# Final norm with sixteen buffers and its loads first; layer 1 projection with an early second load and squares and high parts on two engines

## The chip, the cores and the metric

The kernel runs on one core of one Trainium2 chip. The metric is device time in microseconds (us) of one execution. Before the change it is 3293.6 us, the median of three runs (3292.09 to 3293.63).

## What is computed

A trunk of two layers over 2048 tokens of width 1024 in float32. Layer 0 mixes tokens with causal pooling and a convolution, layer 1 with a chunked gated delta rule over 8 heads; each is followed by a mixture of 32 experts (2 per token). Every sub-layer starts with a normalization whose gain and shift come from a conditioning vector, and the output is normalized once more:

```python
def rmsnorm(x, gain):
    xf = x.astype(jnp.float32)
    y = xf * lax.rsqrt(jnp.mean(xf * xf, axis=-1, keepdims=True) + EPS)
    return (y * gain.astype(jnp.float32)).astype(x.dtype)
...
        mod = (c_act @ mod_w[l] + mod_b[l])[:, None, :]
        sh_m, sc_m, g_m, sh_f, sc_f, g_f = jnp.split(mod, 6, axis=-1)
        hn = rmsnorm(x, norm_mix[l]) * (1.0 + sc_m) + sh_m
...
    return rmsnorm(x, final_norm)
```

In layer 1 the normalized tokens are multiplied with a weight of 1024 x 4112: 4096 columns for queries, keys, values and a gate of 8 heads, and 16 columns for two numbers per head and token.

## The kernel before

The program runs in stages: layer 0's mixer, its experts, layer 1's mixer, its experts, and `final`. Tokens are cut into 16 tiles of 128; four tiles make a chunk of 512, two chunks a half. Float32 products are made from a high part (float32r) and a low part: `split` writes the high part of a tile with a copy on ScalarE (or on VectorE, if told so) and the low part with a subtraction on VectorE, and `proj` multiplies high by high, high by low and low by high.

**Final norm** (`final`, L1038). For each of 16 tiles: load from `acc` (L1045, `xin`, six buffers), square and sum on ScalarE (L1048), mean on VectorE and power on POOL (`rstd`, L187 and L189), scaling by the row's factor and by the gain row `fr` on VectorE (L1050), store (L1051). Loads and stores are issued by SP, which works through its queue in order.

**Layer 1's projection** (`dn_project`, L1130). It has two halves. In each, for both chunks: `norm_x` (L202) loads four tiles of x (L1157, `xin`, four buffers), squares and sums each on ScalarE (L210), takes the power (L189), and scales the tiles on VectorE (L217). `norm_T` (L220) then makes, for each of 8 slices of 128 features, four transposes on TensorE (L229), the scaled and shifted tile `nf` on ScalarE (L231, two buffers), its high part `hh` on ScalarE (L232), its low part `hl` on VectorE (L233). The 16 columns are multiplied at once (L1174), `gates` makes the heads' factors from them, and then come 8 heads (`dn_head`). A head loads four strips of weights (`load_strip`, L244), splits each and multiplies it with both chunks; between the strips `pump` (L1190) advances other work: a triangular inverse, and one block of the modulation (`mod_rest`, L160), which loads 128 rows of its weight (`modw`, L167), multiplies and sums them with the condition on VectorE (L168) and adds a bias (L169). The first call also loads the condition and applies Silu to it. There are 32 such blocks and four calls per head.

The order of instructions on an engine is made by a scheduler of the Tile library from the order of the program and the dependencies, with times of its own. `tc.issue_after(ins)` adds to it: instructions traced in its block are queued behind `ins` if they run on the engine of `ins`. The buffers of the heads' results `na` and `kg` (L1291, L1303) are 8 KB per partition each, in the pool `last`. `first` (L1162) holds the tiles of the third chunk, which `norm_x` prepares ahead of head 7 (L1184).

Of the kernel before, what the change touches and what calls it, by code (L numbers as in the profile page):

```python
# [6 lines left out]
F32 = mybir.dt.float32  # L7
# [63 lines left out]
class Trunk:  # L71
# [127 lines left out]
                nc.tensor.transpose(p[:, j * P:(j + 1) * P], src[:, k:k + 1].to_broadcast([P, P]), self.ident)  # L199
            nc.scalar.activation(out[:, h * 512:(h + 1) * 512], p, AF.Copy)  # L200

    def norm_x(self, l, xload, wk):  # L202

        nc = self.nc
        ss = self.small.tile([P, 4], F32, name="ss")
        xs = []
        for i in range(4):
            x = xload(i)
            sq = wk.tile([P, D], BF16, name="sq", tag="nf", bufs=2)
            nc.scalar.activation(sq, x, AF.Square, accum_out=ss[:, i:i + 1])  # L210
            xs.append(x)
        r = self.rstd(ss, 1.0 / D, 4, "rs")
        for i in range(4):
            if l == 0:
                nc.scalar.activation(xs[i], xs[i], AF.Copy, scale=r[:, i:i + 1])
            else:
                nc.vector.tensor_scalar(xs[i], xs[i], r[:, i:i + 1], None, op0=ALU.mult)  # L217
        return xs

    def norm_T(self, l, which, xs, psum, wk, outs):  # L220

        nc = self.nc
        hh, hl = outs
        g = self.gain[l, which]
        so = l * 48 + (0 if which == 0 else 3) * 8
        for k in range(KD):
            p = psum.tile([P, 512], F32, name="tp")
            for i in range(4):
                nc.tensor.transpose(p[:, i * P:(i + 1) * P], xs[i][:, k * P:(k + 1) * P], self.ident)  # L229
            f = wk.tile([P, 512], F32, name="nf", bufs=2)  # L230
            nc.scalar.activation(f, p, AF.Identity, scale=g[:, k:k + 1], bias=self.mod[:, so + k:so + k + 1])  # L231
            nc.scalar.activation(hh[:, k], f, AF.Copy)  # L232
            nc.vector.tensor_sub(hl[:, k], f, hh[:, k].bitcast(F32))  # L233

    def split(self, h, l, x, eng="act"):
        nc = self.nc
# [801 lines left out]
    def final(self, out, l=1):  # L1038
        tc, nc = self.tc, self.nc
        with tc.tile_pool(name="fin", bufs=3, reuse_waits="tile") as pool:  # L1040
            fr = pool.tile([P, D], F32, name="fr", bufs=1)
            nc.sync.dma_start(fr, self.ins["final"].to_broadcast([P, D]))  # L1042
            for t in range(NT):
                x = pool.tile([P, D], F32, name="xin", bufs=6)
                nc.sync.dma_start(x, self.acc[t * P:(t + 1) * P])  # L1045
                ss = self.small.tile([P, 1], F32, name="ss1")
                sq = pool.tile([P, D], BF16, name="sqo", bufs=1)
                nc.scalar.activation(sq, x, AF.Square, accum_out=ss)  # L1048
                r = self.rstd(ss, 1.0 / D, 1, "rs1")
                nc.vector.scalar_tensor_tensor(x, x, r, fr, op0=ALU.mult, op1=ALU.mult)  # L1050
                nc.sync.dma_start(out[t * P:(t + 1) * P], x)  # L1051
# [78 lines left out]
    def dn_project(self):  # L1130
# [3 lines left out]
        with ExitStack() as ctx:  # L1134
# [24 lines left out]
                return f  # L1159

            self.rest = self.mod_rest(cv, [(1, i) for i in range(16, 48)], tag="modw", bufs=3)
            first = None  # L1162
            for half in range(2):
                hT = []
                ba = cv.tile([P, 8, 16], F32, name="ba", bufs=2)
                for c2 in range(2):
                    hh = hp.tile([P, KD, 512], F32R, name="hh")
                    hl = hp.tile([P, KD, 512], F32R, name="hl")
                    xs = first or self.norm_x(1, xload(half * 2 + c2), wk)
                    first = None  # L1170
                    self.norm_T(1, 0, xs, pst, wk, (hh, hl))
                    hT.append((hh, hl))
                    p = psm.tile([P, 512], F32, name="pm")
                    self.proj(p[:16], (wbh, wbl), (hh, hl))  # L1174
                    bs = wk.tile([16, 512], F32, name="bs", bufs=1)
                    nc.scalar.activation(bs, p[:16], AF.Copy)
                    p = pst.tile([P, 512], F32, name="tp")
                    for i in range(4):
                        nc.tensor.transpose(p[:, i * 16:(i + 1) * 16], bs[:, i * P:(i + 1) * P], self.ident[:16, :16])
                    nc.vector.tensor_copy(ba[:, c2 * 4:c2 * 4 + 4], p[:, :64].rearrange("p (b c) -> p b c", b=4))  # L1180
                beta, g, ex = self.gates(half, ba, cv, pst)
                for hd in range(8):
                    if (half, hd) == (0, 7):
                        first = self.norm_x(1, xload(2), wk)  # L1184
                    self.dn_head(half, hd, hT, beta, g, ex, halo, wp, wk, psm, pst, psk)
                    if hd % 4 == 3:
                        assert next(self.inv, None) is None
                        self.inv = self.dn_invert(half, hd // 4, wk) if (half, hd) != (1, 7) else iter(())

    def pump(self, n):  # L1190

        for _ in range(n):
            next(self.inv, None)
        with self.tc.issue_after(self.loaded.ins):
            next(self.rest, None)

    def dn_head(self, half, hd, hT, beta, g, ex, halo, wp, wk, psm, pst, psk):
        nc, ins = self.nc, self.ins
# [536 lines left out]
```

## Time and profile before

| | |
|---|---|
| Median of three runs | 3293.6 us |
| Profiled execution, its own time | 3291.32 us |
| Its span | 3289.6 us |
| Mean granted TensorE clock | 0.948 |

The profile is of one execution. Times in it count from the start of the span. PE is TensorE (PEld its weight loads), DVE VectorE, ACT ScalarE, POOL GpSimd, SP the engine that issues most DMAs; a q behind a name is the engine's queue. In a timeline a row has start, duration, engine, line, operation, output<-input, shape and count, and in brackets the idle time before it with what ended it.

### The profile page before, as it was taken

The numbers are of one execution on the slowest core, as the hardware profiler recorded it, in microseconds if no ns is written. First come the engines' busy times: TensorE is split into PE (matmuls) and PEld (weight loads), VectorE is DVE, ScalarE is ACT, GpSimd is POOL, SyncE is SP. The second block draws the span as 40 slices with busy tenths as digits, with TensorE's granted clock in tenths as the row PEclk, the third lists the DMA queues.
The fourth block names the chain that finished last, engine by engine and source line by source line (L and its number), as shares of the span: only waits on it lengthen the run. The fifth ranks groups of instructions, "written<-read, shape, count | busy, mean of one in ns | idle before, by whom it ended". The sixth has DMA issues, their size and how long they took to land. (4 is left out here: it accounts for less than half of the span.)

```text
span 3289.6 us, 41913 instructions
## 1 busy us (share of the span) xinstructions
PE 2900.5 (88%) x14192; PEld 2309.4 (70%) x14192; DVE 2435.8 (74%) x3797; ACT 1493.0 (45%) x2559; POOL 1019.7 (31%) x877
## 2 busy tenths in 40 slices
PE   4979888787999996999988999987999996999991
PEld 3756666565777774888876777867897775777770
DVE  4998999767878875768786786877664547888783
ACT  6135233315656655434345343434673224666552
POOL 0142323333444331323222222235540213444441
PEclk9989999888999997999999999988999997999995
DMA  6225243638999864455442434347877537989876
GB/s 223 85 74 208 77 143 115 218 134 276 314 285 304 257 201 151 150 176 179 144 144 93 133 117 141 112 149 215 257 246 225 171 128 253 319 274 299 263 231 219
DMA packets 384985, 633.38 MB, mean 193 GB/s; under 512 B 111232, under 2 KB 245504, under 8 KB 384768
## 3 DMA queue, kind: packets, MB, share of 16 engines
q1 hardware_dynamic: 355904, 563.38, 50.2%
q0 software_dynamic: 28864, 67.30, 8.8%
q8 instruction: 113, 1.85, 0.2%
q14 instruction: 104, 0.85, 0.1%
HBM read 484.46 MB, written 175.44 MB: 201 GB/s over the span
## 5 line engine op out<-in xcount | busy, mean ns | idle before, releaser
L260 PE MATMUL pm<-hh,wh 128*128 128x512 f32 x1408 | 565.9, 402 | 0.8 <-ACT wh L237 0.7
L262 PE MATMUL pm<-hh,wl 128*128 128x512 f32 x1408 | 556.7, 396 | 3.7 <-DVE wl L238 3.7
L261 PE MATMUL pm<-hl,wh 128*128 128x512 f32 x1408 | 555.6, 395 | 4.1 <-DVE hl L233 4.1
L238 DVE TENSOR_TENSOR wl<-wr,wh 128x1024 fp32r<-128x1024 f32 x384 | 452.3, 1219 | 40.7 <-ACT wh L237 37.2
L237 ACT ACTIVATE wh<-wr 128x1024 fp32r<-128x1024 f32 x384 | 399.3, 1057 | 139.8 <-PE pu L828 57.3
L847 POOL DMA_INDIRECT acc<-ys,ixs x102 | 262.2, 2570 | 436.9 <-DVE wl L238 102.6
L261 PEld LDWEIGHTS pm<-hl,wh 128*128 128x128 f32 x1408 | 268.7, 191 | 63.3 <-DVE hl L233 4.5
L260 PEld LDWEIGHTS pm<-hh,wh 128*128 128x128 f32 x1408 | 269.3, 191 | 61.9 <-issue 4.4
L262 PEld LDWEIGHTS pm<-hh,wl 128*128 128x128 f32 x1408 | 268.4, 191 | 62.4 <-DVE wl L238 5.7
L826 PE MATMUL pu<-wh,xt 128*128 128x512 f32 x656 | 268.8, 410 | 0.5 <-ACT xt L237 0.5
L827 PE MATMUL pu<-wl,xt 128*128 128x512 f32 x656 | 261.4, 398 | 0.0
L828 PE MATMUL pu<-wh,xt 128*128 128x512 f32 x656 | 260.4, 397 | 0.0
L238 DVE TENSOR_TENSOR wl<-wraw,wh 128x1024 fp32r<-128x1024 f32 x88 | 111.9, 1271 | 153.5 <-ACT wh L237 153.4
L286 DVE SCALAR_TENSOR_TENSOR acc<-cin,wfir,acc 128x512 f32<-128x512 f32 (+1 forms) x320 | 214.0, 726 | 0.1
L237 ACT ACTIVATE wh<-wraw 128x1024 fp32r<-128x1024 f32 x88 | 93.2, 1059 | 226.2 <-PE pm L261 226.0
L532 PE MATMUL po<-woh,yh 128*128 128x512 f32 x512 | 172.1, 412 | 19.5 <-ACT yh L237 11.0
L1232 DVE SCALAR_TENSOR_TENSOR dacc<-ub,cols,dacc 128x1024 f32<-128x1024 f32 x144 | 186.9, 1298 | 2.8
L532 PE MATMUL po<-wol,yh 128*128 128x512 f32 x512 | 166.7, 406 | 0.0
L532 PE MATMUL po<-woh,yl 128*128 128x512 f32 x512 | 165.9, 403 | 0.3 <-DVE yl L238 0.3
L804 POOL DMA_INDIRECT xg<-hn,ixs x102 | 113.4, 1112 | 160.9 <-PE tp L814 73.9
L828 PEld LDWEIGHTS pu<-wh,xt 128*128 128x128 f32 x656 | 124.2, 189 | 30.6 <-DVE xt L238 0.4
L826 PEld LDWEIGHTS pu<-wh,xt 128*128 128x128 f32 x656 | 124.5, 190 | 28.8 <-ACT xt L237 1.5
(378 smaller groups left out, 6245.7 us busy)
## 6 DMA issues: line engine op xcount, KB each, us to landing
wr<-in_w_up_dram SPq DMA_DIRECT2D x256, 512.0 KB, 7.8
wr<-in_w_down_dram SPq DMA_DIRECT2D x128, 512.0 KB, 7.0
modw<-in_modwT_dram SPq DMA_DIRECT2D x96, 512.0 KB, 5.1
wraw<-in_w_in_dram SPq DMA_DIRECT2D x88, 512.0 KB, 3.6
stin<-stg SPq DMA_DIRECT2D x32, 1280.0 KB, 8.3
yr<-yT SPq DMA_DIRECT2D x32, 512.0 KB, 4.4
acc<-xo SPq DMA_DIRECT2D x32, 512.0 KB, 3.0
hn<-ho SPq DMA_DIRECT2D x32, 512.0 KB, 3.6
```

Of the source, the lines that this page charges most:

```text
L237: a = nc.scalar.activation(h, x, AF.Copy) if eng == "act" else nc.vector.tensor_copy(h, x)
L238: return a, nc.vector.tensor_sub(l, x, h.bitcast(F32))
L260: nc.tensor.matmul(ps, wh[:, k], hh[:, k], start=k == 0, stop=False)
L261: nc.tensor.matmul(ps, wh[:, k], hl[:, k], start=False, stop=False)
L262: nc.tensor.matmul(ps, wl[:, k], hh[:, k], start=False, stop=k == KD - 1)
L286: self.tap = nc.vector.scalar_tensor_tensor(o, x, w, i, op0=ALU.mult, op1=ALU.add)
L532: nc.tensor.matmul(ps[:, ns], a[:, k], b[:, ns], start=k == 0 and i == 0, stop=k == KD - 1 and i == 2)
L826: nc.tensor.matmul(ps, xh[:, k], uh, start=k == 0, stop=False)
L827: nc.tensor.matmul(ps, xh[:, k], ul, start=False, stop=False)
L828: nc.tensor.matmul(ps, xl[:, k], uh, start=False, stop=k == KD - 1)
L847: st = nc.gpsimd.indirect_dma_start(out=self.acc, out_offset=bass.IndirectOffsetOnAxis(ap=ix[:, 0:1], axis=0), in_=ys, in_offset=None, bou ...
L1232: nc.vector.scalar_tensor_tensor(acc, ub[:, i:i + 1024], self.col("dn_conv", si * 4 + i), acc, op0=ALU.mult, op1=ALU.add)
```

## The change

Three parts. `final` gets 16 buffers for `xin`, and all 16 loads are issued ahead of the loop that squares, scales and stores. `norm_x` can put some of its squares on VectorE; layer 1 does so for the tiles 1 and 3 of its first, second and fourth chunk, and `norm_T` makes the high part of every second slice of layer 1 on VectorE. `dn_project` loads the second chunk's four tiles into the buffers of `kg` and `na`, in a block behind the last square that is on ScalarE; the second and the fourth chunk are normalized where they are used, as before, the third ahead of head 7. `pump` leaves the modulation alone in head 0.

```diff
--- before.py
+++ after.py
@@ -199,7 +199,8 @@
                 nc.tensor.transpose(p[:, j * P:(j + 1) * P], src[:, k:k + 1].to_broadcast([P, P]), self.ident)
             nc.scalar.activation(out[:, h * 512:(h + 1) * 512], p, AF.Copy)
 
-    def norm_x(self, l, xload, wk):
+    def norm_x(self, l, xload, wk, dve=()):
+
 
         nc = self.nc
         ss = self.small.tile([P, 4], F32, name="ss")
@@ -207,7 +208,10 @@
         for i in range(4):
             x = xload(i)
             sq = wk.tile([P, D], BF16, name="sq", tag="nf", bufs=2)
-            nc.scalar.activation(sq, x, AF.Square, accum_out=ss[:, i:i + 1])
+            if i in dve:
+                nc.vector.scalar_tensor_tensor(sq, x, 1.0, x, op0=ALU.mult, op1=ALU.mult, accum_out=ss[:, i:i + 1])
+            else:
+                self.squared = nc.scalar.activation(sq, x, AF.Square, accum_out=ss[:, i:i + 1])
             xs.append(x)
         r = self.rstd(ss, 1.0 / D, 4, "rs")
         for i in range(4):
@@ -229,8 +233,7 @@
                 nc.tensor.transpose(p[:, i * P:(i + 1) * P], xs[i][:, k * P:(k + 1) * P], self.ident)
             f = wk.tile([P, 512], F32, name="nf", bufs=2)
             nc.scalar.activation(f, p, AF.Identity, scale=g[:, k:k + 1], bias=self.mod[:, so + k:so + k + 1])
-            nc.scalar.activation(hh[:, k], f, AF.Copy)
-            nc.vector.tensor_sub(hl[:, k], f, hh[:, k].bitcast(F32))
+            self.split(hh[:, k], hl[:, k], f, "dve" if l and k % 2 else "act")
 
     def split(self, h, l, x, eng="act"):
         nc = self.nc
@@ -1040,9 +1043,12 @@
         with tc.tile_pool(name="fin", bufs=3, reuse_waits="tile") as pool:
             fr = pool.tile([P, D], F32, name="fr", bufs=1)
             nc.sync.dma_start(fr, self.ins["final"].to_broadcast([P, D]))
+            xs = []
             for t in range(NT):
-                x = pool.tile([P, D], F32, name="xin", bufs=6)
+                x = pool.tile([P, D], F32, name="xin", bufs=NT)
                 nc.sync.dma_start(x, self.acc[t * P:(t + 1) * P])
+                xs.append(x)
+            for t, x in enumerate(xs):
                 ss = self.small.tile([P, 1], F32, name="ss1")
                 sq = pool.tile([P, D], BF16, name="sqo", bufs=1)
                 nc.scalar.activation(sq, x, AF.Square, accum_out=ss)
@@ -1159,16 +1165,28 @@
                 return f
 
             self.rest = self.mod_rest(cv, [(1, i) for i in range(16, 48)], tag="modw", bufs=3)
-            first = None
+            def xlate(i):
+
+                if i % 2 == 0:
+                    pairs.append(self.last.tile([P, 2, D], F32, name="xlate", tag=("kg", "na")[i // 2], bufs=1))
+                x = pairs[-1][:, i % 2]
+                nc.sync.dma_start(x, self.x2[(4 + i) * P:(5 + i) * P])
+                return x
+
+            pairs = []
+            ready = {0: self.norm_x(1, xload(0), wk, (1, 3))}
+            with tc.issue_after(self.squared.ins):
+                late = [xlate(i) for i in range(4)]
             for half in range(2):
                 hT = []
                 ba = cv.tile([P, 8, 16], F32, name="ba", bufs=2)
                 for c2 in range(2):
                     hh = hp.tile([P, KD, 512], F32R, name="hh")
                     hl = hp.tile([P, KD, 512], F32R, name="hl")
-                    xs = first or self.norm_x(1, xload(half * 2 + c2), wk)
-                    first = None
-                    self.norm_T(1, 0, xs, pst, wk, (hh, hl))
+                    c = half * 2 + c2
+                    if c % 2:
+                        ready[c] = self.norm_x(1, late.__getitem__ if c == 1 else xload(c), wk, (1, 3))
+                    self.norm_T(1, 0, ready.pop(c), pst, wk, (hh, hl))
                     hT.append((hh, hl))
                     p = psm.tile([P, 512], F32, name="pm")
                     self.proj(p[:16], (wbh, wbl), (hh, hl))
@@ -1181,7 +1199,8 @@
                 beta, g, ex = self.gates(half, ba, cv, pst)
                 for hd in range(8):
                     if (half, hd) == (0, 7):
-                        first = self.norm_x(1, xload(2), wk)
+                        ready[2] = self.norm_x(1, xload(2), wk)
+                    self.heads = half * 8 + hd
                     self.dn_head(half, hd, hT, beta, g, ex, halo, wp, wk, psm, pst, psk)
                     if hd % 4 == 3:
                         assert next(self.inv, None) is None
@@ -1191,8 +1210,9 @@
 
         for _ in range(n):
             next(self.inv, None)
-        with self.tc.issue_after(self.loaded.ins):
-            next(self.rest, None)
+        if self.heads:
+            with self.tc.issue_after(self.loaded.ins):
+                next(self.rest, None)
 
     def dn_head(self, half, hd, hT, beta, g, ex, halo, wp, wk, psm, pst, psk):
         nc, ins = self.nc, self.ins
```

## Rows read from the trace of the kernel before

**Rows 1.** The page, part 1: engine, busy us, share of the span, instructions.

```profile
PE 2900.5 (88%) x14192; PEld 2309.4 (70%) x14192; DVE 2435.8 (74%) x3797; ACT 1493.0 (45%) x2559; POOL 1019.7 (31%) x877
```

**Rows 2.** Timeline of SP's queue, final norm: start, duration, instruction.

```profile
3226.57 1.98 SPq L1045 DMA_DIRECT2D xin<-acc  x4
3235.59 6.35 SPq L1051 DMA_DIRECT2D out_dram<-xin  x4
3241.98 2.27 SPq L1045 DMA_DIRECT2D xin<-acc  x4
...
3279.70 6.54 SPq L1051 DMA_DIRECT2D out_dram<-xin  x4
```

**Rows 3.** Timeline of all engines in the final norm.

```profile
3232.25 1.06 ACT L1048 ACTIVATE sqo<-xin 128x1024 bf16<-128x1024 f32 x1 [16.01 <-DMA xin<-acc]
...
3233.58 1.06 ACT L1048 ACTIVATE sqo<-xin 128x1024 bf16<-128x1024 f32 x1 [0.18 <-DMA xin<-acc]
...
3234.28 1.28 DVE L1050 SCALAR_TENSOR_TENSOR xin<-xin,rs,fr 128x1024 f32<-128x1024 f32 x1 [0.69 <-POOL rs L189]
...
3240.30 1.28 DVE L1050 SCALAR_TENSOR_TENSOR xin<-xin,rs,fr 128x1024 f32<-128x1024 f32 x1 [0.66 <-POOL rs L189]
...
3284.59 1.28 DVE L1050 SCALAR_TENSOR_TENSOR xin<-xin,rs,fr 128x1024 f32<-128x1024 f32 x1 [0.72 <-POOL rs L189]
```

**Rows 4.** Table, final norm: stretch, us, busy us by engine, PEclk, DMA share, GB/s.

```profile
3232.00:3234.00 2.00, 0.00 (x0) 0.00 (x0) 0.15 (x1) 1.57 (x3) 0.33 (x1) 0.50 1.04 422
...
3236.00:3238.00 2.00, 0.00 (x0) 0.00 (x0) 1.35 (x2) 1.15 (x3) 0.54 (x2) 0.50 0.65 262
...
3242.00:3244.00 2.00, 0.00 (x0) 0.00 (x0) 0.00 (x0) 0.00 (x0) 0.00 (x0) 0.50 0.83 266
```

**Rows 5.** Table by stretches, opening of layer 1's projection.

```profile
1260.00:1270.00 10.00, 9.27 (x42) 5.19 (x40) 8.91 (x17) 9.24 (x16) 0.00 (x0) 0.78 0.79 265
1270.00:1280.00 10.00, 3.34 (x16) 1.58 (x15) 4.26 (x11) 5.17 (x10) 1.01 (x1) 0.73 0.40 157
```

**Rows 6.** Timeline of SP's queue, opening.

```profile
1244.58 1.85 SPq L1157 DMA_DIRECT2D xin<-acc  x4
...
1267.06 23.93 SPq L1157 DMA_DIRECT2D xin<-acc  x8
```

**Rows 7.** Timeline of all engines, opening.

```profile
1252.67 1.06 ACT L210 ACTIVATE sq<-xin 128x1024 bf16<-128x1024 f32 x1
...
1258.56 1.45 ACT L231 ACTIVATE nf<-tp,mod,gain 128x512 f32<-128x512 f32 x2 [1.28 <-PE tp L229]
...
1259.90 1.14 ACT L232 ACTIVATE hh<-nf 128x512 fp32r<-128x512 f32 x2
...
1280.92 1.45 ACT L231 ACTIVATE nf<-tp,mod,gain 128x512 f32<-128x512 f32 x2 [4.70 <-PE tp L229]
...
1283.71 1.45 ACT L231 ACTIVATE nf<-tp,mod,gain 128x512 f32<-128x512 f32 x2 [0.30 <-DVE hl L233]
1283.95 0.63 PE L260 MATMUL pm<-hh,wh 128*128 128x512 f32 x1
```

**Rows 8.** VectorE's groups, 1240 to 1760: us busy, mean ns, idle before.

```profile
L238 DVE TENSOR_TENSOR wl<-wraw,wh 128x1024 fp32r<-128x1024 f32 x34 | 41.7, 1225 | 73.6 <-ACT wh L237 73.6
L168 DVE SCALAR_TENSOR_TENSOR modw<-modw,cact 128x1024 f32<-128x1024 f32 x32 | 39.1, 1222 | 1.9 <-DMA modw<-in_modwT_dram 1.9
...
L233 DVE TENSOR_TENSOR hl<-nf,hh 128x512 fp32r<-128x512 f32 x32 | 20.7, 688 | 17.8 <-ACT hh L232 17.7
...
L217 DVE TENSOR_SCALAR xin<-xin,rs 128x1024 f32<-128x1024 f32 x16 | 11.2, 750 | 4.4 <-POOL rs L189 4.4
...
L168 DVE DVE_READ_ACCUMULATOR modw<-modw,cact 128x1 f32 x32 | 2.7, 84 | 0.0
```

**Rows 9.** Table by stretches, a late stretch of the first half's heads.

```profile
1642.00:1699.00 57.00, 48.87 (x229) 40.07 (x228) 51.31 (x60) 20.79 (x31) 12.85 (x11) 0.94 0.41 133
```

**Rows 10.** Timeline of SP's queue at the turn of the halves.

```profile
1731.49 1.82 SPq L1157 DMA_DIRECT2D xin<-acc  x4
```

## The prediction

> **What bounds the kernel now.** I read the page first: TensorE is busy for 88% of the span [rows 1]. That is an average over stages, and the diff touches three places where TensorE has nothing to do or little: the final norm, the opening of layer 1's projection, and the turn between its two halves. Each is read by itself, the queue of SP first, then the timeline of the engines, then a table by stretches.
>
> The final norm runs in four rounds. SP issues four loads, then four stores, then the next four loads, up to four last stores [rows 2]: the first round is 15.4 us long (loads at 3226.57 and 3241.98), the last stores go out from 3279.70. In a round the first square waits for its load (3232.25, 5.7 us after the first issue), and then the scalings follow each other at (3240.30 - 3234.28) / 3 = 2.0 us [rows 3], since VectorE takes mean, power on POOL and scaling of one tile before it turns to the next. So neither DMA nor VectorE is the bound: they take turns. The table shows it [rows 4]: 422 GB/s with the DMA engines full while loads land, 262 GB/s at a share of 0.65 while stores go out one by one.
>
> The opening of layer 1 has TensorE busy for 9.3 us of 10 and then 3.3 of 10 [rows 5], at a granted clock of 0.78 and 0.73 of full speed. The reason is in SP's queue [rows 6]: the loads of the second 512 tokens (the first four of the eight) go out at 1267.06, when the buffers of the first come free. In the timeline [rows 7] the first chunk's last square begins at 1252.67, its first scaled-and-shifted tiles (nf) are made at 1258.56, and those of the second chunk only at 1280.92. The strips' matmuls begin at 1283.95. What happens ahead of them sets when the whole half begins.
>
> **The change, part by part.**
>
> *Final norm.* Sixteen buffers and loads first take the turns away. What is left is the longer of two paths. The compute path: the first scaling stays at 3234.28, and fifteen pitches of 2.0 us put the last at 3264.4 where it now is at 3284.59 [rows 3], 20 us earlier, the order on VectorE being unchanged. The DMA path: 512 KB for the gain row, 16 loads and 16 stores of 512 KB are 17.3 MB. The full slice moved 422 GB/s at a share of 1.04 [rows 4], so 406 GB/s at a share of one, and 17.3 MB take 42.6 us. Counted from 3227.5 they end at 3270.1; the last scaling now ends at 3285.9, 3.7 us ahead of the end of the span, and of this I take the half for the last landing and the end of the program. So the span would end near 3272. DMA is the later path, so 17.5 us are gained. The sixteen issues take SP 16 x 0.5 = 8 us, until 3234.6 at four in 1.98 [rows 2], before the first store is due. The stores then stand behind loads that SP issued before them, which costs nothing while the sum of the bytes is the bound. Bounds: 20 us if the compute path alone counts; 6 us if loads and stores that mix move only the 266 GB/s at a share of 0.83 of the slice where both ran [rows 4], that is 320 GB/s, 54 us in place of 42.6.
>
> The Trainium skill, "DMA: Bandwidth & Descriptors", Specifications, gives a limit of about 358 GB/s for one core at HBM; by it the bytes would take 48.3 us, an estimate, and the gain would be 12 us. The trace disagrees in the slice of loads alone, which moved 422 GB/s [rows 4], and the measurement decides.
>
> *Opening: the loads of the second chunk.* They get their own place in the buffers of kg and na, which head 0 writes only after its strips, so their release costs nothing. The diff puts them in an issue_after block on a square; as it is used elsewhere in the kernel, this queues instructions of the engine of the instruction named, here ScalarE, and these four DMAs are SP's. I read them as going out right behind the first four, at about 1246.5 [rows 6]. Landing one behind the other at the 1.3 us between loads in the final norm (3232.25 and 3233.58, squares that wait for theirs [rows 3]), the eight tiles are there by about 1258. The two weight strips that SP issues behind them are late by 4 x 0.46 us of issue and about 5 us of transfer; nobody needs them before the strips' matmuls, at about 1270, so they stay hidden.
>
> *Opening: less on the path.* The modulation of head 0 goes away: four products of 1.22 us and their readouts of 0.08 us on VectorE [rows 8], 5.2 us, with a small addition each, that now lie among the first chunk's work, a Silu with its table load on ScalarE, and five DMAs on SP. They come back in head 8, a stretch like those of the other heads; the tightest stretch of the heads is late in the half [rows 9], VectorE 51.3 of 57 us, and that one already has them.
>
> *Opening: what VectorE gets.* Two squares per chunk, same form as the modulation's product, 1.22 + 0.08 us each [rows 8]; on ScalarE one takes 1.06 us and a readout [rows 7]. For the first chunk I gain nothing: its fourth square started without waiting at 1252.67, but by the spacing its tile landed only just before, so VectorE would finish it as late. Four copies of 128x512 per chunk in place of ScalarE's 0.57 us (a pair in 1.14 [rows 7]): the trace has no such copy. Below it cannot be less than half of the scaling of 128x1024 (0.750 us, so 0.38), above not more than the two-source subtraction of the same shape (0.69) [rows 8]. It is nearest to the scaling, one source in SBUF, so I take 0.45. ScalarE's work on a chunk, four pairs of 1.45 and 1.14 us, falls from 10.4 to 8.1 us, but with two buffers for nf a tile still goes through scaling, high part and subtraction before its buffer is free; in the order in which ScalarE now does them, two nf and then the high parts, a pair would take some 2.65 us where it now takes 2.8 (1280.92 to 1283.71). I count 1 us per chunk, bounds 0 and 2.4.
>
> *Opening: the sum.* From 1258.2 VectorE has for the first chunk eight subtractions (5.5 us) and four copies (1.8), for the second two squares (2.6) and four scalings (3.0), and one weight strip (1.2): 14.1 us, until about 1272. So the second chunk's nf begins at about 1271 in place of 1280.92 [rows 7]: 10 us. From there the work of TensorE is as before, and it moves up as a whole. Bounds: 13 us, if the squares fall into the holes before 1258 and a pair takes 2.1 us; 2 us, if work of the third chunk, whose buffers now come free at about 1267, is put between (four squares of 1.06 us, four scalings of 0.75).
>
> *Turn of the halves.* The loads for the fourth chunk go out at 1731.49, when SP has worked off the stores of head 7, not when the buffers come free [rows 10]. VectorE's squares and the copies shorten what lies between, but a load that starts at most 0.5 us earlier is waited for. I take 1 us, bounds 0 and 4.
>
> Sum: 17.5 + 10 + 1 = 28.5 us. The profiled execution took 3291.3 us (a span of 3289.6), so 3262.8; the median of the runs shown lies 2.3 us above it, so I predict **3265 us**. Best ends together: 20 + 13 + 4 = 37, 3257. Worst: 6 + 2 + 0 = 8, 3286.
>
> **The rivals.**
>
> *Mixed transfers are slower.* For: the slice with both kinds had a share of 0.83 at 266 GB/s [rows 4]; against: its share was not one, and the store-only slice gives 262 / 0.65 = 403 GB/s. The final stage gains 6 us: 3276.5. (By the Trainium skill's limit of 358 GB/s, named above, it would gain 12: 3271.)
>
> *VectorE takes the opening's gain.* For: 14 us of its work in a stretch of 14; it now has 8.91 us of 10 there [rows 5]. Then the second chunk begins near 1279: 3273.
>
> *The change doesn't do what it says: the loads of the second chunk do wait for the square.* They would be issued at about 1252.5 and land until 1262, in time for a slightly later square: 2 us, 3267. Were the weight strips held behind them, they would land at 1264, still before their use.
>
> *Slower.* One mechanism: sixteen loads in flight with the stores behind them lower the DMA rate of the final stage itself. It decides when 17.3 MB take over 61.5 us (now) + 11 (gained before) + 6.6 us, that is below 219 GB/s; at 200 GB/s the stage takes 86.5 us and the kernel 3307. Every slice in the rows is above that [rows 4].
>
> **How the numbers follow.** Forecast 0.62, mixed transfers 0.13, VectorE 0.12, waiting loads 0.08: all faster by more than 0.2% (6.6 us, about what a measurement of this kernel can tell from no change), 0.95. Two losses together, 8 us gained and so at that limit, 0.03, which I count as the same; the slow DMA 0.02. The range reaches from the best ends to a point between the two single losses and both: 3257 to 3279.
>
> **What would show it.** In the changed profile: SP with 16 loads in a row, squares at the landing pitch of 1.3 us, scalings at 2.0 us, DMA full for some 43 us from the first load on; eight loads of x ahead of the first weight strip; no modulation before head 1; the second chunk's nf at about 1271. It is wrong if the final stage still takes over 55 us, or if that nf begins after 1277.

## The result, and the profile after

The changed kernel takes 3275.0 us (median of five runs, 3269.4 to 3281.6) beside 3293.6 us of the kernel before in the same comparison: a ratio of 0.9944, 95% interval 0.9928 to 0.9959. That is 18.6 us faster where 28.5 us were forecast; the time lies inside the predicted range.

Where the gain comes from is read from three anchors that both kernels have: SP's issue of the 16 columns' weight (`wba`), which opens layer 1's projection, SP's issue of the final gain row (`fr`), and the end of the span. The profiled executions have spans of 3289.6 and 3273.3 us, 16.3 us apart. From `fr` to the end it was 63.42 us (3289.6 less 3226.18) and is 45.81 (3273.3 less 3227.49): 17.6 us. From `wba` to `fr`, which holds the whole of layer 1's mixer and its experts, it was 1981.99 us and is 1981.76: 0.2 us. The changed execution came to `wba` 1.5 us later (1245.73 in place of 1244.19), in code that the change doesn't touch. So in these two executions the final norm is the whole gain, and the projection gave nothing in sum.

**The final norm.** SP's queue in the changed kernel, which answers to [rows 2]:

```profile
3227.49 0.34 SPq L1045 DMA_DIRECT2D fr<-in_final_dram  x1
3227.88 14.57 SPq L1049 DMA_DIRECT2D xin<-acc  x16
3243.47 24.09 SPq L1057 DMA_DIRECT2D out_dram<-xin  x16
```

Sixteen loads stand in a row, and no store stands between them. Each issue now takes 14.57 / 16 = 0.91 us where four took 1.98 us together. The scalings on VectorE, first and last of 16, as in [rows 3]:

```profile
3235.08 1.28 DVE L1056 SCALAR_TENSOR_TENSOR xin<-xin,rs,fr 128x1024 f32<-128x1024 f32 x1 [0.69 <-POOL rs L189]
...
3265.91 1.28 DVE L1056 SCALAR_TENSOR_TENSOR xin<-xin,rs,fr 128x1024 f32<-128x1024 f32 x1 [0.72 <-POOL rs L189]
```

Their pitch is (3265.91 - 3235.08) / 15 = 2.06 us, and the last one ends 6.1 us ahead of the end of the span, so they are not the bound. They stand close behind it: with the 3.7 us that lay between the last scaling's end and the end of the span before, they alone would end the span at 3270.9, an estimate, only 2.4 us sooner. The table by stretches shows the bound, with the columns of [rows 4]:

```profile
3229.00:3231.00 2.00, 0.00 (x0) 0.00 (x0) 0.00 (x0) 0.00 (x0) 0.00 (x0) 0.50 0.89 254
3231.00:3233.00 2.00, 0.00 (x0) 0.00 (x0) 0.00 (x0) 0.00 (x0) 0.00 (x0) 0.50 0.99 383
...
3243.00:3245.00 2.00, 0.00 (x0) 0.00 (x0) 1.35 (x2) 1.75 (x5) 0.47 (x2) 0.50 1.04 414
...
3263.00:3265.00 2.00, 0.00 (x0) 0.00 (x0) 1.28 (x3) 0.00 (x0) 0.54 (x1) 0.50 1.03 422
...
3231.00:3271.00 40.00, 0.00 (x0) 0.00 (x0) 21.67 (x32) 18.38 (x32) 8.68 (x16) 0.50 1.02 414
```

For 40 us the DMA engines are full, at a mean of 414 GB/s, through loads alone (the second row), loads and stores mixed (the third) and stores alone (the fourth). The Trainium skill, "DMA: Bandwidth & Descriptors", Specifications, has about 358 GB/s for one core; its section Measured says that its own figures, up to 425 GB/s, are of a single core with the other core of the pair idle, and that with both streaming each gets roughly 358. The kernel runs on one core, and the 414 GB/s over 40 us agrees with that section.

**The opening of the projection.** The changed kernel's timeline, SP first, then ScalarE and VectorE; it answers to [rows 6, 7]:

```profile
1246.12 1.85 SPq L1163 DMA_DIRECT2D xin<-acc  x4
1248.02 2.31 SPq L1173 DMA_DIRECT2D xlate<-acc  x4
1250.37 17.68 SPq L251 DMA_DIRECT2D wraw<-in_w_in_dram  x3
...
1260.58 1.45 ACT L235 ACTIVATE nf<-tp,mod,gain 128x512 f32<-128x512 f32 x2 [6.17 <-PE tp L233]
...
1270.26 0.64 ACT L240 ACTIVATE hh<-nf 128x512 fp32r<-128x512 f32 x1
1271.65 1.06 ACT L214 ACTIVATE sq<-xlate 128x1024 bf16<-128x1024 f32 x1 [0.75 <-ACT hh L240]
...
1279.77 1.45 ACT L235 ACTIVATE nf<-tp,mod,gain 128x512 f32<-128x512 f32 x2 [5.31 <-PE tp L233]
...
1257.21 2.74 DVE L221 TENSOR_SCALAR xin<-xin,rs 128x1024 f32<-128x1024 f32 x4 [1.17 <-POOL rs L189]
1262.06 0.43 DVE L240 CAST hh<-nf 128x512 fp32r<-128x512 f32 x1 [2.11 <-ACT nf L235]
...
1272.20 1.23 DVE L212 SCALAR_TENSOR_TENSOR sq<-xlate 128x1024 bf16<-128x1024 f32 x1
```

The second chunk's loads (`xlate`) go out right behind the first chunk's, 2.3 us after `wba`; before, they went out 22.9 us after it [rows 6], so they are 20.6 us sooner. But the squares of these tiles run only at 1271.65 and 1272.20, behind the first chunk's last high part, and VectorE stood idle for 2.11 us ahead of 1262.06 meanwhile. The second chunk's first `nf` comes 34.0 us after the issue of `wba`; before it was 36.7 (1280.92 in [rows 7] less 1244.19).

**The turn of the halves.** GpSimd's gate products (`gm`: the first four are head 8's, the next two head 9's), the matmuls on TensorE that wait for them, VectorE beside them, and the table by stretches, all of the changed kernel:

```profile
1768.16 1.04 POOL L1277 TENSOR_TENSOR gm<-upper,gh 128x512 fp32r<-128x512 f32 x1 [25.73 <-PE pm L265]
1769.15 2.02 POOL L1277 TENSOR_TENSOR gm<-upper,gl 128x512 fp32r<-128x512 f32 x1
...
1771.27 1.52 POOL L1277 TENSOR_TENSOR gm<-upper,gh 128x512 fp32r<-128x512 f32 x1
1772.75 2.01 POOL L1277 TENSOR_TENSOR gm<-upper,gl 128x512 fp32r<-128x512 f32 x1
...
1774.82 0.79 PE L1279 MATMUL tk<-gm,slower_r 128*128 128x512 f32 x1 [1.25 <-POOL gm L1277]
...
1768.99 1.28 DVE L241 TENSOR_TENSOR wl<-wraw,wh 128x1024 fp32r<-128x1024 f32 x1 [0.73 <-ACT wh L240]
...
1770.00:1775.00 5.00, 2.07 (x7) 0.78 (x6) 4.93 (x5) 0.05 (x1) 5.00 (x5) 0.89 0.38 111
1775.00:1780.00 5.00, 5.00 (x12) 3.94 (x13) 2.79 (x2) 3.37 (x3) 4.90 (x4) 0.50 0.00 0
```

The same four products and the same stretch in the kernel before:

```profile
1768.78 1.04 POOL L1257 TENSOR_TENSOR gm<-upper,gh 128x512 fp32r<-128x512 f32 x1 [26.48 <-DVE gh L1099]
1769.78 1.04 POOL L1257 TENSOR_TENSOR gm<-upper,gl 128x512 fp32r<-128x512 f32 x1
1770.90 1.90 POOL L1257 TENSOR_TENSOR gm<-upper,gh 128x512 fp32r<-128x512 f32 x1
1772.76 1.03 POOL L1257 TENSOR_TENSOR gm<-upper,gl 128x512 fp32r<-128x512 f32 x1
...
1770.00:1775.00 5.00, 3.50 (x14) 2.04 (x13) 4.89 (x4) 1.62 (x5) 4.92 (x5) 1.00 0.38 111
```

Before, TensorE was busy for 3.50 us of these five, and its granted clock stayed at 1.00, the 2.4 GHz level. After the change the second and the fourth take twice as long and the third 1.52 us, TensorE is busy for 2.07 us of the five, and in the next five the granted clock is 0.50, the 1.2 GHz level.

The heads show what each of these is worth. Take as the end of a head the start of its v transposes' input on ScalarE (`vT`), counted from `wba`: head 0 ended at 94.4 us and ends at 93.1, head 7 at 468.8 and 466.8, head 8 at 559.9 and 561.6. The opening gained 1.3 us, and from head 7 to head 8 it now takes 94.9 us in place of 91.1.

### The profile page after: what moved, and what is told of

Read it like the earlier page. It is cut to its first block, busy times and chain, and to the rows that moved or that the text cites. A ratio compares the mean times of both kernels' runs of the same rounds, so it can differ in the third digit from the quotient of the medians.

```text
span 3273.3 us, 41914 instructions
## 1 busy us (share of the span) xinstructions
PE 2902.6 (89%) x14192; PEld 2309.0 (71%) x14192; DVE 2445.1 (75%) x3825; ACT 1476.1 (45%) x2529; POOL 1025.9 (31%) x877
## 5 line engine op out<-in xcount | busy, mean ns | idle before, releaser
L264 PE MATMUL pm<-hl,wh 128*128 128x512 f32 x1408 | 556.0, 395 | 4.1 <-DVE hl L241 4.1
L241 DVE TENSOR_TENSOR wl<-wraw,wh 128x1024 fp32r<-128x1024 f32 x88 | 109.2, 1240 | 156.8 <-ACT wh L240 156.7
```

Of the source, the lines that this page charges most:

```text
L241: return a, nc.vector.tensor_sub(l, x, h.bitcast(F32))
L264: nc.tensor.matmul(ps, wh[:, k], hl[:, k], start=False, stop=False)
```

## The experiments

All kernels compute the whole reference. Their milestones, from one profiled execution of each, in us from the issue of `wba`; the ratio is to the kernel before in the same comparison, with its 95% interval, where it was timed in five rounds. "Again" is the same kernel run anew.

| kernel | second chunk's first nf | head 0 | head 7 | head 7 to 8 | head 8 | ratio |
|---|---|---|---|---|---|---|
| before | 36.7 | 94.4 | 468.8 | 91.1 | 559.9 | 1 |
| after | 34.0 | 93.1 | 466.8 | 94.9 | 561.6 | 0.9944 (0.9928 to 0.9959) |
| after, again | 33.3 | 91.6 | 466.0 | 94.8 | 560.8 | 0.9952 (0.9935 to 0.9968) |
| final norm alone | 36.7 | 94.5 | 468.8 | 91.4 | 560.1 | 0.9931 (0.9917 to 0.9945) |
| final norm alone, again | 36.3 | 94.3 | 468.9 | 91.4 | 560.2 | 0.9935 (0.9917 to 0.9954) |
| buffers alone | 36.6 | 94.4 | 467.9 | 91.9 | 559.8 | |
| projection alone | 33.4 | 93.5 | 467.1 | 95.4 | 562.5 | 1.0005 (0.9996 to 1.0014) |
| squares ahead | 33.1 | 90.6 | 465.3 | 94.9 | 560.2 | 0.9942 (0.9928 to 0.9956) |
| own scratch | 32.1 | 89.6 | 464.4 | 95.1 | 559.5 | 0.9943 (0.9930 to 0.9957) |
| squares ahead, on ScalarE | 30.3 | 87.8 | 461.2 | 94.8 | 556.0 | |
| the same, again | 30.2 | 87.6 | 460.9 | 95.1 | 555.9 | 0.9933 (0.9913 to 0.9953) |
| modulation in head 0 | 37.6 | 95.9 | 470.1 | 92.7 | 562.8 | |
| second half as before | 33.4 | 91.6 | 465.9 | 91.5 | 557.4 | |
| both mends | 30.5 | 88.0 | 462.3 | 91.6 | 554.0 | 0.9908 (0.9891 to 0.9924) |

Behind head 8 single executions differ by more than these effects: the kernel before took 1422.1 us from there to `fr`, and the run with buffers alone (below), with the same code up to the final norm, 1428.6. So parts of the projection are compared by milestones.

The milestones have a spread of their own. Four kernels have the projection of before: head 0 ends at 94.3 to 94.5 us in them, and the turn takes 91.1 to 91.9. Four executions have the changed kernel's opening (both of the changed kernel, projection alone, second half as before): their `nf` comes at 33.3 to 34.0 us and head 0 ends at 91.6 to 93.5, so the opening gained 0.9 to 2.9 us.

### Which part of the change gains

Final norm alone: the kernel before with the new `final`.

```diff
+            xs = []
             for t in range(NT):
-                x = pool.tile([P, D], F32, name="xin", bufs=6)
+                x = pool.tile([P, D], F32, name="xin", bufs=NT)
                 nc.sync.dma_start(x, self.acc[t * P:(t + 1) * P])
+                xs.append(x)
+            for t, x in enumerate(xs):
```

> The kernel before with the new final norm alone. My account of the result: the final stage, from its first load's issue to the end of the span, took 63.0 us before and 45.4 after, and that 17.6 us is nearly the whole gain; so this kernel gains 17.5 us (16 to 19), its final stage takes 45.5 us and its DMA engines stand at 95% or more for 40 us. Rival (the gain of the whole change needs the earlier projection as well, or the final gains less by itself): a gain under 14 us, or a final stage over 48 us.

Its ratio is 0.9931, 3272.7 us against 3296.6: 24 us by the medians, 18 to 27 by the interval, more than the 17.5 expected. Its final stage, from its first load (3225.10) to the end of the span (3271.0), takes 45.9 us, and the middle 40 us read:

```profile
3229.00:3269.00 40.00, 0.00 (x0) 0.00 (x0) 21.67 (x32) 18.39 (x32) 8.68 (x16) 0.50 1.02 411
```

The stage does what was expected; the surplus over 17.5 us isn't in it, and no run shows where it comes from. The repeat's interval, 15 to 27 us, holds 17.5.

Projection alone: the changed kernel with the old `final`.

```diff
-                x = pool.tile([P, D], F32, name="xin", bufs=NT)
-                xs.append(x)
-            for t, x in enumerate(xs):
+                x = pool.tile([P, D], F32, name="xin", bufs=6)
```

> The change without the new final norm: layer 1's projection alone. My account: the opening gives 1.7 us by the end of head 0, the turn of the halves takes some 3.7 back, and what is left by the last stage is 0 to 1 us, so the time is that of the kernel before within 2 us. Rival (the projection is worth the 10 us that I forecast for it, and the run-to-run spread hid it): 8 us or more faster.

The ratio is 1.0005 (0.9996 to 1.0014): nothing gained or lost, to within 5 us. The 10 us of the forecast are excluded.

Buffers alone: the kernel before with sixteen buffers and its loads where they were.

```diff
-                x = pool.tile([P, D], F32, name="xin", bufs=6)
+                x = pool.tile([P, D], F32, name="xin", bufs=NT)
```

> The kernel before with 16 x buffers in the final norm and nothing else: each load stays beside its own scaling and store in the loop, and the order on SP's queue is the same as before. Theory Q (in the kernel before the loads of each batch stood behind the stores of the batch before, and those wait for the scalings: the order on the queue is the bound): the final stage stays at 60 to 63 us, batches of four as before. Rival N (the six buffers were the bound, and the order is of no account): 46 to 52 us.

SP's queue in that run:

```profile
3232.41 2.05 SPq L1045 DMA_DIRECT2D xin<-acc  x4
3241.61 6.35 SPq L1051 DMA_DIRECT2D out_dram<-xin  x4
3248.00 2.28 SPq L1045 DMA_DIRECT2D xin<-acc  x4
```

The next four loads still wait behind four stores, the rounds are 15.6 us long (15.4 in [rows 2]), and from the first load to the end of the span (3296.0) it takes 63.6 us, against 63.0 before: 0.6 us over the range expected, and no gain. Buffers without the new order are worth nothing. That order without buffers was not tried: sixteen loads ahead of the loop need sixteen.

### Why the opening gained so little

Two runs free the second chunk's squares. One writes its `norm_x` ahead of the first chunk's `norm_T`:

```diff
             with tc.issue_after(self.squared.ins):
                 late = [xlate(i) for i in range(4)]
+            ready[1] = self.norm_x(1, late.__getitem__, wk, (1, 3))
...
-                    if c % 2:
-                        ready[c] = self.norm_x(1, late.__getitem__ if c == 1 else xload(c), wk, (1, 3))
+                    if c == 3:
+                        ready[c] = self.norm_x(1, xload(c), wk, (1, 3))
```

> The change with the squares and the scaling of the second 512 tokens written ahead of the first 512's transposes, so that their scratch takes its buffers before the gain-and-shift tiles do. Theory 1 (the squares came late, because their scratch shares two buffers with those tiles and stands behind them in the order): the squares run from about 1259 to 1262, the second chunk's first gain-and-shift tile comes 25 to 28 us after the issue of the wba load (34.0 in the changed kernel, 36.7 before), and head 0 ends 6 to 9 us sooner. Rival 1 (the data are late, or VectorE and ScalarE are full until then): it stays at 33 to 35 us and nothing is gained. Rival 2 (the tiles come sooner and the gates or the weight strips swallow it): the tile at 25 to 28 us, head 0's end within 2 us of the changed kernel's.

The other leaves the order of the program and gives these squares another scratch than the two buffers that `nf` uses too:

```diff
-    def norm_x(self, l, xload, wk, dve=()):
+    def norm_x(self, l, xload, wk, dve=(), own=False):
...
-            sq = wk.tile([P, D], BF16, name="sq", tag="nf", bufs=2)
+            sq = wk.tile([P, D], BF16, name="sq", **(dict(tag=("sqk", "kd")[i % 2], bufs=1) if own else dict(tag="nf", bufs=2)))
...
-                        ready[c] = self.norm_x(1, late.__getitem__ if c == 1 else xload(c), wk, (1, 3))
+                        ready[c] = self.norm_x(1, late.__getitem__ if c == 1 else xload(c), wk, (1, 3), own=c == 1)
```

> The change with its program order kept, and other buffers for the second chunk's squares alone (two borrowed ones, in place of the two that the gain-and-shift tiles also use). Theory 1 (the shared buffers put the squares late): as in the run that moves the squares ahead, the second chunk's first tile at 25 to 28 us from the wba load, head 0's end 6 to 9 us sooner than in the changed kernel, and some 6 us off the whole. Rival 1 (data or engines late): 33 to 35 us and nothing gained. Rival 3 (the place in the program's order decides, not the buffer): this run stays at 33 to 35 while the run with the squares ahead gains.

In both the squares run early. ScalarE and VectorE of the run with a scratch of its own:

```profile
1253.32 1.06 ACT L214 ACTIVATE sq<-xlate 128x1024 bf16<-128x1024 f32 x1 [1.27 <-DMA xlate<-acc]
...
1260.11 1.05 ACT L214 ACTIVATE sq<-xlate 128x1024 bf16<-128x1024 f32 x1
...
1276.34 1.45 ACT L235 ACTIVATE nf<-tp,mod,gain 128x512 f32<-128x512 f32 x2 [1.10 <-PE tp L233]
...
1257.53 1.22 DVE L212 SCALAR_TENSOR_TENSOR sq<-xlate 128x1024 bf16<-128x1024 f32 x1
```

So it was the shared scratch that held them, not late data, and the place in the program was not needed. But the `nf` behind them moved by 0.9 and 1.9 us only, to 33.1 and 32.1, where theory 1 had 25 to 28 (by 0.2 and 1.2 us against the earliest of the four executions with the changed opening); the times of the whole did not move. Half of theory 1 held, and its rival of full engines took the rest. In the run with the squares ahead, VectorE is busy for 14.31 of the 17 us from 1257 to 1274.

The next run takes 2.5 us of it to ScalarE, which has gaps:

```diff
-            ready[1] = self.norm_x(1, late.__getitem__, wk, (1, 3))
+            ready[1] = self.norm_x(1, late.__getitem__, wk)
```

> The change with the second chunk's squares ahead of the first chunk's transposes, and all four of them on ScalarE instead of two on VectorE. In the run that only moved them ahead, VectorE was busy for nearly all of the time from 1257 to 1273.6, and the second chunk's first gain-and-shift tile came 33.1 us after the issue of the wba load (34.0 in the changed kernel). Theory V (VectorE's own work is now the bound of the opening): with 2.5 us of it moved to an engine that has gaps, that tile comes at 30.0 to 31.5 us, and head 0 ends 1.5 to 3 us sooner than the 90.6 of that run. Rival E (the chain of bs, its transposes and the first transposes of the second chunk behind it on TensorE is the bound): 32.5 to 33.5 us, and nothing gained.

ScalarE, then VectorE, in that run:

```profile
1256.18 1.06 ACT L214 ACTIVATE sq<-xlate 128x1024 bf16<-128x1024 f32 x1
...
1271.73 0.59 ACT L1195 ACTIVATE bs<-pm 16x512 f32<-16x512 f32 x1 [1.92 <-PE pm L265]
1273.41 1.45 ACT L235 ACTIVATE nf<-tp,mod,gain 128x512 f32<-128x512 f32 x2 [1.09 <-PE tp L233]
...
1258.66 2.74 DVE L221 TENSOR_SCALAR xlate<-xlate,rs 128x1024 f32<-128x1024 f32 x4 [1.13 <-POOL rs L189]
...
1270.31 0.69 DVE L241 TENSOR_TENSOR hl<-nf,hh 128x512 fp32r<-128x512 f32 x1
```

The `nf` comes at 30.3 us and head 0 ends at 87.8, 2.8 us sooner than with the squares ahead alone, both within what theory V expected: VectorE was the bound there. What is left shows in the rows. The last subtraction of the first chunk ends at 1271.00, and the `nf` follows 2.4 us behind it, over the last products of the 16 columns, their copy `bs`, its transposes and the second chunk's transposes on TensorE. Its time was 38 us below that of the kernel before beside it. By the anchors, against the profiled execution of before, 9.8 us of that lie between `wba` and `fr` (1972.2) and 17.7 behind `fr` (45.7). Most of the rest is the kernel before itself, whose execution beside it took 3300.9 us where the profiled one took 3291.3; the timed repeat found 0.9933, 23 us by the medians.

One run puts the modulation back into head 0:

```diff
-        if self.heads:
-            with self.tc.issue_after(self.loaded.ins):
-                next(self.rest, None)
+        with self.tc.issue_after(self.loaded.ins):
+            next(self.rest, None)
```

> The change with one step undone: head 0 works on the remaining modulation again, as before. Theory T (the turn of the halves loses because VectorE's weight residual and GpSimd's gate products now start within half a microsecond of each other, and GpSimd loses): the moved modulation has no part in it, so from head 7's v transposes to head 8's it takes 93 to 95 us as in the changed kernel (94.9; 91.1 before), and head 0 ends within 1.5 us of the changed kernel's 93.1 from the wba load. Rival M (the modulation that was moved out of head 0 into head 8 costs the 3.7 us): 91 to 92 us at the turn.

Both numbers missed. Head 0 ends at 95.9 us, 2.8 us later than in the changed kernel (4.3 later than in its repeat) and 1.5 later than before: in this one execution, without that move the opening would have lost time. And the turn takes 92.7 us, between the two theories. Its order on TensorE, in the next part, fits that.

### Why the turn lost

The second half as before: no squares of its chunks on VectorE, all high parts on ScalarE.

```diff
-    def norm_T(self, l, which, xs, psum, wk, outs):
+    def norm_T(self, l, which, xs, psum, wk, outs, dve=False):
...
-                        ready[c] = self.norm_x(1, late.__getitem__ if c == 1 else xload(c), wk, (1, 3))
-                    self.norm_T(1, 0, ready.pop(c), pst, wk, (hh, hl))
+                        ready[c] = self.norm_x(1, late.__getitem__ if c == 1 else xload(c), wk, () if c == 3 else (1, 3))
+                    self.norm_T(1, 0, ready.pop(c), pst, wk, (hh, hl), c < 2)
...
-            self.split(hh[:, k], hl[:, k], f, "dve" if l and k % 2 else "act")
+            self.split(hh[:, k], hl[:, k], f, "dve" if dve and k % 2 else "act")
```

> The change with the second half's squares and high parts on ScalarE again, as before; the first half stays changed. In this kernel 15 matmuls of the next strip stand ahead of the last 512 tokens' gates on TensorE as before, where the changed kernel has 17. Theory T (those two matmuls free a weight buffer 0.4 us sooner, the residual on VectorE meets the gate products on GpSimd earlier, and GpSimd's take 2.02 us in place of 1.04): the turn takes 90.5 to 92 us again, four or more of the six gate products at the start of head 8 at most 1.1 us, TensorE's clock stays at 1.00 there, and the loss of 3.7 us is gone, though the 2 us that the changed half 1 gained ahead of the gates are given up. Rival S (any earlier start of the gates loses it): 94 to 95 us and five products at 2.02.

The turn takes 91.5 us, the loss is gone, and the clock is 1.00 in every stretch from 1760 to 1785. What was expected to be given up was not: the first gate product starts 522.1 us after `wba`, in the changed kernel 522.4. So the second half's squares and copies on VectorE gained nothing ahead of the gates, and the turn takes 3.3 us more with them (94.85 less 91.53). The modulation that went into head 8 is still there in this run, so rival M is out as the cause.

Both mends together: the squares ahead and on ScalarE, and the second half as before (the edits above).

> Both mends together: the second chunk's squares ahead of the first chunk's transposes and all on ScalarE (as in the run that brought head 0's end to 87.8 us from the wba load), and the second half's squares and high parts as before (as in the run whose turn of the halves took 91.5 us). If the two add up: head 0 ends at 87.5 to 88.5, head 8 at 551.5 to 553.5 (559.9 before, 561.6 in the changed kernel), and the whole is 24 to 31 us faster than the kernel before, ratio 0.9905 to 0.9927. Rival (the turn's matmul order goes with the opening, or the later heads swallow the gain): head 8 at 555 or later.

GpSimd, VectorE, the high part `wh` on ScalarE that `wl` waits for, and the table at its turn:

```profile
1764.63 1.04 POOL L1278 TENSOR_TENSOR gm<-upper,gh 128x512 fp32r<-128x512 f32 x1 [26.06 <-DVE gh L1105]
1765.63 1.04 POOL L1278 TENSOR_TENSOR gm<-upper,gl 128x512 fp32r<-128x512 f32 x1
1766.75 1.90 POOL L1278 TENSOR_TENSOR gm<-upper,gh 128x512 fp32r<-128x512 f32 x1
1768.61 1.04 POOL L1278 TENSOR_TENSOR gm<-upper,gl 128x512 fp32r<-128x512 f32 x1
...
1765.92 1.83 DVE L241 TENSOR_TENSOR wl<-wraw,wh 128x1024 fp32r<-128x1024 f32 x1 [1.17 <-ACT wh L240]
...
1764.83 1.06 ACT L240 ACTIVATE wh<-wraw 128x1024 fp32r<-128x1024 f32 x1 [4.57 <-PE pm L264]
...
1765.00:1770.00 5.00, 3.49 (x17) 2.07 (x16) 4.08 (x3) 1.85 (x4) 4.92 (x5) 1.00 0.19 51
1770.00:1775.00 5.00, 5.00 (x23) 4.10 (x22) 4.89 (x4) 2.31 (x2) 5.00 (x4) 1.00 0.15 61
```

The same `wh` in the changed kernel, and `wl` with the modulation in head 0:

```profile
1767.90 1.06 ACT L240 ACTIVATE wh<-wraw 128x1024 fp32r<-128x1024 f32 x1 [4.57 <-PE pm L264]
...
1773.05 2.06 DVE L241 TENSOR_TENSOR wl<-wraw,wh 128x1024 fp32r<-128x1024 f32 x1 [0.95 <-ACT wh L240]
```

The pair of rows to compare is VectorE's `wl` and the second product. With both mends `wl` starts 1.29 us after the first product (1765.92 less 1764.63), when the second, at 1.00 us, is under way: the product takes 1.04 us and `wl` 1.83. In the changed kernel `wl` starts 0.83 us after the first product, ahead of the second: the product takes 2.02 us and `wl` 1.28. With the modulation in head 0 it starts 1.06 us after, just behind the second product, which takes 1.04, and `wl` 2.06; there only the later products are long, and the turn is in the middle, at 92.7. On TensorE 15, 16 and 17 matmuls of the next strip stand ahead of the last chunk's gates in the runs with 1.29, 1.06 and 0.83: two matmuls at 0.23 us each set `wl`'s start, since it waits for `wh`, and `wh` for a product that frees its buffer (the brackets of the rows above). All fourteen executions fall into these three groups: 1.29 us and a turn of 91.1 to 91.9 in six, 1.06 and 92.7 in one, 0.83 or 0.84 and 94.8 to 95.4 in seven. No run moves `wl` by itself.

The Trainium skill, "SBUF — State Buffer", section "SBUF: two separate sides", says that VectorE and GpSimd share one pair of ports, and that of a VectorE instruction with two inputs from SBUF and a GpSimd instruction that reads SBUF the one that starts first holds the pair for its whole instruction while the other waits. By it, with the 1.22 us [rows 8] and the 1.04 us that the two take alone, `wl` would take 1.97 us with both mends and the changed kernel's second product 2.16, estimates; they took 1.83 and 2.02, so the rows agree to 0.14 us.

TensorE's clock is a part of the loss that these products don't settle alone. It fell behind them in all seven executions with 0.83, but also once where they were short, in the run with buffers alone:

```profile
1766.56:1771.56 5.00, 3.56 (x17) 2.09 (x15) 3.82 (x4) 2.03 (x4) 4.92 (x5) 1.00 0.18 33
1771.56:1776.56 5.00, 4.93 (x15) 3.93 (x16) 4.89 (x4) 2.31 (x2) 5.00 (x5) 0.66 0.20 79
```

In the kernel before, the same ten us from the first product on have TensorE busy for 3.56 and 4.93 us as well, and the clock is 1.00 in both halves. Why it fell in one and not in the other stays open.

The whole of both mends is 0.9908 (0.9891 to 0.9924), 3265.9 us against 3296.4, 30.5 us faster, and head 8 ends at 554.0, half a microsecond past the expected range. For the comparison three kernels ran beside it.

> The kernel of the second chunk's squares ahead and on ScalarE, timed now: its single look was 38 us below the kernel before in the same call, of which the heads' milestones bear out 7 (head 15) and the final norm 17.5. By milestones it is 22 to 27 us faster than before; a gain over 33 us would mean that something after the heads changed with it.

> The changed kernel once more, beside the others on the same chip: 0.9928 to 0.9959 of the kernel before, as measured first. If the milestones count, it is 4 to 8 us slower than the run with both mends and 3 to 6 slower than the run with the second chunk's squares ahead.

> The kernel before with the new final norm alone, once more, beside the whole change on the same chip. If the projection part is worth nothing as a whole, this and the changed kernel agree within their spread (a difference of under 4 us); if the projection part costs something after all, this one is the faster by 3 us or more.

The changed kernel's repeat is 0.9952 (0.9935 to 0.9968), and that interval lies wholly above that of both mends: this version beats both kernels. The medians are 13 us apart, where the milestones explain 7 at head 8. The final norm alone is 0.9935 (0.9917 to 0.9954) and the squares ahead on ScalarE 0.9933 (0.9913 to 0.9953): by the intervals these two and the changed kernel can't be told apart. But beside each other the final norm alone is 4.3 us faster than the changed kernel by the medians (3275.0 and 3279.2), and five of its six times lie below all of the changed kernel's. That leans to the projection part costing something as it stands; head 8 has only 0.6 us of it, so the question stays open. Against the final norm alone, both mends are 9.1 us faster by the medians, of which head 8 shows 6; their intervals overlap by 0.0007.

## Why the prediction was right, and where not

*Final norm, 17.5 us:* right, 17.6 measured. The DMA path is the bound as worked out, and mixed transfers are no slower, which ends that rival and the slower case. Off was the price of the issues, 0.91 us each and not 0.5, so that the first store went out at 3243.47, 7.1 us after its scaling had ended (3236.36). It cost nothing, because the DMA engines had loads to move until then.

*Opening, 10 us:* wrong; 1.3 us at head 0's end, 2.9 in the repeat. By the prediction's own sign it is wrong too, as the second chunk's `nf` begins at 1279.77, after 1277. The loads did go out behind the first four, and the copy on VectorE took 0.43 us where 0.45 was taken; a pair takes 2.75 us, not 2.65, where it took 2.79 before (1280.92 to 1283.71), so the copies gained next to nothing. The step that failed is "From 1258.2 VectorE has ... 14.1 us, until about 1272. So the second chunk's nf begins at about 1271". It sums an engine's work as if each piece could run when its data are there. The squares could not: their scratch is the pair of buffers of `nf`, and in the program's order the first chunk has it first. That was to be read in the kernel before. With the scratch apart, the sum was still short: it had one weight strip where two run, no wait for POOL's power (1.13 us), and no chain over `bs` on TensorE (2.4 us). With the best order tried, `nf` came 6.4 us sooner than before. The rival "VectorE takes the opening's gain" named 1279 and 3273 us; the run came to 1279.8 and 3275.0. Its cause was second in line: the buffers first, and VectorE behind them. That its numbers came so near is in part luck: 1.5 us of the 1279.8 are the later start at `wba`, and its 3273 still holds the 1 us of the turn that turned out a loss.

*Modulation out of head 0:* counted as part of the opening with no price; it is worth 2.4 to 4.3 us there, by one execution without the move (95.9 us at head 0's end) against four with it (91.6 to 93.5).

*Turn of the halves, 1 us, bounds 0 and 4 of gain:* wrong in sign, 3.7 us lost. The step looked at the loads alone and left out that work moved on TensorE and VectorE meets GpSimd elsewhere. In the profiled execution the loss adds up: from the first gate product to the matmul of the fourth it took 5.07 us and takes 6.66 (1774.82 less 1768.16), 1.6 us more; then 12 matmuls at the 1.2 GHz level take 5.1 us where 0.23 us each make 2.8, 2.4 us more. The 1.6 us stand in all seven executions with 17 matmuls, the rest falls differently: in the other six head 8 ends 37.9 to 38.1 us behind the first product (39.2 here, 35.35 before), and the first product itself comes 56.7 to 57.4 us after head 7's end (55.65 here, 55.8 before). What delays it there is not shown.

In sum, of 28.5 us the 17.5 were right, the 10 were 1 to 3, and the 1 was -3.7; what is left to the 0.2 us between `wba` and `fr` lies behind head 8, inside the spread. The forecast's sign and its range held because the one large term was right.

## What to carry to other kernels

Before work is counted as moved up, look for what it shares: a scratch tile that takes its buffers in the program's order holds an instruction back as surely as its data do. A queue in which stores wait for compute and loads stand behind them is mended by order and buffers together; buffers alone did nothing. And after a change that moves work by half a microsecond, look again at the places where VectorE and GpSimd run beside each other on TensorE's path.

## What was not expected of the hardware

A start 0.46 us sooner on VectorE turned GpSimd's second and fourth 128x512 products from 1.04 to 2.02 us. TensorE's clock can differ where its work doesn't: with the same busy time in two stretches of five us (3.56 and 4.93), the second had a granted clock of 1.00 in one execution and 0.66 in another, which cost 1.6 us (36.9 us from the first product to head 8's end in place of 35.35). With 16 loads of 512 KB in a row SP needs 0.91 us for an issue where it needs 0.5 for four, and the DMA engines hold a mean of 414 GB/s for 40 us through loads, mixed loads and stores, and stores.
